# A fourth 7-product unit for the gates, and two pieces of stick-breaking attention moved off VectorE

## The chip, the cores and the metric

The kernel runs on one core of a Trainium2 chip. The metric is the device time of one execution in microseconds (us), the median of three runs: 1687.3 us before the change, 1686.08 to 1689.03. The engines are named as in the profile: PE is TensorE's matmul, PEld its weight load, DVE is VectorE, ACT is ScalarE, POOL is GpSimd, and SP is SyncE, which here only issues DMAs.

## The reference

One decoder block over 1024 tokens of width 1024. From the normed input `h`, one wide projection gives everything that attention needs, and the logits of three gates:

```
proj = einsum('bsd,de->bse', h, w_in)          # columns: sb q,k,v | fox q,k,v | f | mem q | 3 x 1024 gate logits
o_sb  = stick_breaking_attention(...)          # 8 heads of 64
o_fox = forgetting_attention(...)              # 8 heads of 64
o_mem = memory_attention(...)                  # 4 heads of 128, over 256 memory tokens
gates = sigmoid(gate_logit)                    # three of (1024 tokens, 1024)
merged = gates0 * (o_sb @ Wb_sb) + gates1 * (o_fox @ Wb_fox) + gates2 * (o_mem @ Wb_mem)
x = x + merged @ w_out                         # then a squared-ReLU MLP, 1024 -> 4096 -> 1024
```

Stick-breaking attention is strictly causal. With `z = q.k / 8`, the weight of token s for query t is `sigmoid(z[t,s])` times the product of `1 - sigmoid(z[t,j])` over s < j < t, and zero for s >= t:

```
log_rem = where(strict, log_sigmoid(-z), 0);  after = reverse_cumsum(log_rem) - log_rem
w = where(strict, exp(log_sigmoid(z) + after), 0);  out = w @ v
```

Everything is float32. The kernel splits each operand of a product into a high and a low part and multiplies in two or three passes.

## The kernel before

*The order of work.* Up to the end of attention the order is not written out by hand. A planner inside the program (`Machine`, line 184) plays the kernel through when it is built: every piece of work is an `Op` with an engine and an estimated cost, every buffer a place that a `Get` waits for, and each engine takes the ready piece with the smallest due time. What it picks is emitted at once, so each engine's instructions stand in a fixed order. Pieces marked `side=True` come only when nothing else is ready on their engine: on PE these are the 7-product units, the dense gates and the branch products. DMAs are issued by SP and POOL in the same way.

*The projection.* Six projections (stick-breaking k, q and v, memory q, forgetting k and q) and the gates in `GATES` run as 7-product units (`unit_products`, `unit_evict`, line 1456): a block of 512 columns of `w_in` against both token halves is computed by Strassen's scheme with 7 half-size products instead of 8. Each product is 2 halves x 4 k x 3 passes of matmuls over 512 columns. The weight blocks' sums and splits are made by `unit_prep` (lines 1386, 1054, 1055). `GATES` holds three units: row blocks 16 to 19, 20 to 23 and 0 to 3, of 24 blocks of 128 gate columns. The units stand one behind the other in `PROJ`.

*The dense gates.* Gate blocks that are in no unit and not computed earlier run as dense tasks (`gates`, line 1811; matmuls at line 1144): blocks 4 to 7 and 10 to 15, each 2 token halves x 8 k x 3 passes. Each needs one weight block split by ACT (line 1054) and DVE (line 1055), and two evictions with a sigmoid (line 1637, a plain copy for blocks 8 to 15). All gates are stored to `gate_scr`. These tasks follow the units and are the side work of PE while attention runs.

*Attention.* Attention begins when the last unit's products are issued (`second_part`, event `ready`). Four pairs of stick-breaking heads come first, then four pairs of forgetting heads; memory attention begins after the first pair. A head's query rows are taken in four units of two 128-row tiles. For a stick-breaking tile (`sb_tile`), per chunk of up to 512 keys: PE makes the scores into one of two score banks (lines 823, 824), on the chunk with the diagonal DVE adds a mask of 1e30 to the last 128 columns in the bank (line 834), ACT takes two sigmoids of the bank, `rho` and `beta` (lines 827, 828), and DVE scans from the right, `state = rho * state + beta`, in place over `beta` (line 843). The scores are negated, so a masked column has rho 1 and beta 0. In `unit`, PE turns the weights (line 917), ACT and DVE split them (lines 922, 924), and PE multiplies with a stationary operand that holds the high and the low part of v side by side (line 934). The result has 128 rows: 64 with the products of one part of v and 64 with those of the other. Forgetting heads copy all 128 rows out and store the halves apart, to `o_scr[1]` and `low_scr`; stick-breaking heads copy 64 rows (line 962), add the other 64 on DVE (line 963) and store one half (line 965).

*The branches.* `dense_branch` multiplies the stored attention outputs with the branch weights, also at line 1144: memory first, then stick-breaking, and the forgetting branch after the planned part. Its operands are fetched by `fetched_o` (line 1659) into tiles of the ring `RR` and split by `bring`. The memory branch's operands wait for the end of memory attention (`mem_over`); the stick-breaking ones for the loads of the last pair, and two of them for the end of the memory branch. For the forgetting branch `fetched_o` also loads the low half and the row sums. `RR` has three tiles, two of them lent to stick-breaking attention until its four pairs are over, and gets four more when all pairs are over.

Of the kernel before, what the change touches and what calls it, by code (L numbers as in the profile page):

```python
# [27 lines left out]
HD = 64  # L28
# [15 lines left out]
def tile_hybrid_block(  # L44
# [20 lines left out]
    nc = tc.nc  # L65
# [20 lines left out]
    dram = ctx.enter_context(tc.tile_pool(name="dram", bufs=1, space=bass.MemoryType.DRAM))  # L86
# [24 lines left out]
        nc.scalar.activation(C.t("st", [P, 8])[:, :1], one, AF.Sqrt)  # L111
    root_table()
    o_scr = [dram.tile([512, S], F32, name=f"o_scr{b}", tag=f"o_scr{b}") for b in range(3)]
    low_scr = dram.tile([512, S], F32, name="low_scr", tag="low_scr")
    l_scr = dram.tile([8, S], F32, name="l_scr", tag="l_scr")
    gate_scr = dram.tile([3 * D, S], F32, name="gate_scr", tag="gate_scr")
    fq_scr = dram.tile([8, 4, S], F32, name="fq_scr", tag="fq_scr")
# [219 lines left out]
    holder = {}  # L337
# [6 lines left out]
    def banks(tag):  # L344
        return Places([bank(tag) for _ in range(PSB[tag])])
# [4 lines left out]
    PP, SC, TR, PV = (banks(tag) for tag in ("pp", "sc", "tr", "pv"))  # L350
    ES, OO, EL, RR, HT, PH, PL, OB, VV, BK, LATER, NONE, RQ = (Places([]) for _ in range(13))
# [460 lines left out]
    def sb_tile(pair, b, i, beta):  # L812
        n = P * (i + 1)
        q = pair.t["q", b, i // 4][:, (i % 4) * P:(i % 4 + 1) * P]
        ch = chunks(i)
        scanned = Event()

        def chunk(ci, c, m, u):
            rho = yield Get(RQ)
            sc = yield Get(SC)  # L820

            def scores():
                nc.tensor.matmul(sc[:, :m], q, pair.t["k1", b, ci][:, :m], start=True, stop=False)
                nc.tensor.matmul(sc[:, :m], q, pair.t["k2", b, ci][:, :m], start=False, stop=True)

            def sigmoids():
                nc.scalar.activation(rho[:, :u], sc[:, :u], AF.Sigmoid, scale=HD ** -0.5)
                nc.scalar.activation(beta[:, c:c + u], sc[:, :u], AF.Sigmoid, scale=-HD ** -0.5)  # L828

            yield Op("PE", 2 * mm_time(max(m, 256)), scores)  # L830
            last = c + u == n
            if last:
                dg = sc[:, u - P:u]
                yield Op("DVE", 0.22, lambda: nc.vector.tensor_tensor(
                    dg, dg, holder["later"][:, 385:513], ALU.add))
            yield Op("ACT", act_time(u, u), sigmoids, table=AF.Sigmoid)
            SC.put(sc)
            if not last:
                yield scanned

            def scan():
                back = beta[:, c:c + u][:, ::-1]
                nc.vector.tensor_tensor_scan(out=back, data0=rho[:, :u][:, ::-1], data1=back,  # L843
                                             initial=0.0 if last else beta[:, c + u:c + u + 1],
                                             op0=ALU.mult, op1=ALU.add)
# [42 lines left out]
    def unit(pair, b, g, es):  # L888
# [2 lines left out]
        for ev in [spawn(tile_(pair, b, 2 * g + a, es[a]), 0.5 * a) for a in range(2)]:  # L891
            yield ev
        pair.read(b, g)
        scr, r0 = o_scr[0 if pair.kind == "sb" else 1], (2 * pair.p + b) * HD
        js = list(range(2 * g + 1, -1, -1))
        turned, pv, started = [], [None], Event()
        products = [Event() for _ in range(g + 2)]
# [51 lines left out]
            yield ev  # L949
        ob = yield Get(OB)  # L950
        rows, cols = slice(r0, r0 + HD), slice(g * 256, (g + 1) * 256)
        if pair.kind == "fox":
            yield Op("ACT", act_time(256), lambda: nc.scalar.activation(ob, pv[0][:, :256], AF.Copy))
            PV.put(pv[0])

            def halves():
                nc.sync.dma_start(scr[rows, cols], ob[:HD, :])
                nc.sync.dma_start(low_scr[rows, cols], ob[HD:, :])
            yield Op("SP", 0.2, halves, 3.0)
        else:  # L960
            o = ob[:HD, :]
            yield Op("ACT", act_time(256), lambda: nc.scalar.activation(o, pv[0][HD:P, :256], AF.Copy))
            yield Op("DVE", dve_time(256), lambda: nc.vector.tensor_tensor(o, o, pv[0][0:HD, :256], ALU.add))
            PV.put(pv[0])
            yield Op("SP", 0.1, lambda: nc.sync.dma_start(scr[rows, cols], o), 2.5)
        OB.put(ob)
        pair.units += 1
        if pair.units == 8:
# [383 lines left out]
        machine.fire(forgot)  # L1352

    KINDS = ("P1", "P2", "P6", "P7", "P5", "P3", "P4")
    GATES = {"ga": 16, "gb": 20, "gc": 0}
    PROJ = ("sbk", "sbq", "mq", "fxk", "fxq", "sbv", *GATES)
    COLS = {**{u: C_G + n * P for u, n in GATES.items()}, "sbv": C_SBV, "mq": C_MQ, "fxk": C_FXK, "fxq": C_FXQ, "sbk": C_SBK, "sbq": C_SBQ}
    prepped, p_ops, landed_ = ({(u, kind): Event() for u in PROJ for kind in KINDS} for _ in range(3))
# [160 lines left out]
    def unit_final(u, ct, q, src, of_bank=False):  # L1519

        c, t = ct
        if u == "sbv":
# [135 lines left out]

    def fetched_o(bi, k):

        raw_ = yield Get(RR)
        raw, rows = raw_[:, :S], slice(k * P, (k + 1) * P)
        yield from transfer(lambda: nc.sync.dma_start(raw, o_scr[order[bi][1]][rows, :]), P * S * 4)
        if bi == 2:
            t = yield Get(RR)
            yield from transfer(lambda: nc.sync.dma_start(t, low_scr[rows, :]), P * S * 4)
            yield Sleep(1.0 if k == ks[3] else 2.0)
            yield Op("DVE", dve_time(S), lambda: nc.vector.tensor_tensor(raw, raw, t, ALU.add))
# [278 lines left out]
    for s in range(0, ST, 2):  # L1947
        t = RA.t("h", [P, 2, D])
# [3 lines left out]
    gb = N.t("gb", [P, D])  # L1952
# [54 lines left out]
    sb = []  # L2007
# [34 lines left out]
    with tc.manual_schedule():  # L2042
# [79 lines left out]
        rows = [], []  # L2122
# [598 lines left out]
```

## Time and profile before

| | us |
|---|---|
| runs: median, lowest, highest | 1687.3, 1686.08, 1689.03 |
| profiled execution, first to last instruction | 1686.7 |
| PE busy | 1675.3 |
| DVE, ACT, POOL busy | 1293.0, 848.9, 255.2 |
| last 7-product unit | 441.7 to 480.6 |
| stick-breaking and memory attention | 480.6 to 719 |
| forgetting attention | 719 to 877.8 |
| stick-breaking branch | 877.8 to 922.5 |

The profile is of one execution; its time is its span, which lies within the runs. Times in it count from its first instruction. Busy time of a group is the union of its instructions, so groups whose matmuls overlap can't be added; a number behind an x is a count. An idle time is put down to what ended it.

### The profile page before, as it was taken

What the parts mean: (1) busy time and instruction counts of PE and PEld (TensorE: products, weight loads), DVE (VectorE), ACT (ScalarE), POOL (GpSimd) and SP (SyncE); (2) the same over time, 40 slices, a digit from 0 to 9 for tenths busy, and PEclk for the clock granted to TensorE, in tenths of its full rate; (3) what the DMA queues carried; (4) which work ended last, traced back from release to release, by engine and by line L of the source; (5) the groups of instructions that cost most, each with busy time, mean ns of one, the idle gap of its engine ahead of it and who ended that gap; (6) DMA issues with size and microseconds to landing.
All of it is one profiled execution on the core that took longest, in us unless ns stands there. A gap on an engine that the chain in (4) does not pass through costs nothing.

```text
span 1686.7 us, 25003 instructions
## 1 busy us (share of the span) xinstructions
PE 1675.3 (99%) x9118; PEld 1432.0 (85%) x9118; DVE 1293.0 (77%) x2079; ACT 848.9 (50%) x1474; POOL 255.2 (15%) x440
## 2 busy tenths in 40 slices
PE   9999999999999999999999999999999999999999
PEld 9998899998888888888888887878888887888887
DVE  7977778855459888867877898987777776688775
ACT  6455555534358888866761446433333344332331
POOL 0000000000253151254400011022111120000000
PEclk9999999999999999999999999999999999999999
DMA  7445434467475365387747542144444484564532
GB/s 245 157 150 182 149 119 150 146 194 243 127 232 161 111 186 151 117 240 224 236 146 245 183 162 100 57 162 155 152 150 137 150 307 171 202 202 143 198 125 75
DMA packets 142221, 284.32 MB, mean 169 GB/s; under 512 B 16913, under 2 KB 53329, under 8 KB 142098
## 3 DMA queue, kind: packets, MB, share of 16 engines
q1 hardware_dynamic: 110562, 183.08, 32.0%
q0 software_dynamic: 31536, 99.64, 19.5%
q8 instruction: 72, 1.18, 0.3%
q14 instruction: 51, 0.42, 0.1%
HBM read 189.83 MB, written 92.83 MB: 168 GB/s over the span
## 4 chain that ended last, share of the span: by engine, by line
PE 92%; DVE 5%; DMA 2%; ACT 1%; issue 1%; SPq 0%; DVEq 0%; ACTq 0%
PE pp L1456 11%; PE pp L1144 10%; PE pp L1981 10%; PE pp L2658 8%; PE sc L1456 7%; PE sc L1144 6%; PE sc L1981 5%; PE sc L2658 4%; PE tr L2658 4%; PE tr L917 4%; PE pv L1456 3%; PE pv L2658 3%; PE tr L1981 2%; PE sc L934 2%; PE pp L934 2%; DVE h L1917 1%
## 5 line engine op out<-in xcount | busy, mean ns | idle before, releaser
L1055 DVE TENSOR_TENSOR wlo<-raw,whi 128x1024 fp32r<-128x1024 f32 (+1 forms) x88 | 107.5, 1222 | 80.2 <-ACT whi L1054 80.0
L1054 ACT ACTIVATE whi<-raw 128x1024 fp32r<-128x1024 f32 (+1 forms) x88 | 93.2, 1059 | 78.8 <-PE pp L1456 32.7
L2658 PE MATMUL pp<-h,sop 128*128 128x512 f32 x540 | 128.4, 396 | 0.0
L2658 PEld LDWEIGHTS pp<-h,sop 128*128 128x128 f32 x540 | 101.6, 188 | 24.4
L1981 PE MATMUL pp<-h,oh 128*128 128x512 f32 x384 | 121.1, 397 | 0.7 <-ACT cu L2066 0.6
L924 DVE TENSOR_TENSOR ptl<-tr,pth 128x512 fp32r<-128x512 f32 (+1 forms) x160 | 99.1, 628 | 24.1 <-ACT pth L922 23.1
L922 ACT ACTIVATE pth<-tr 128x512 fp32r<-128x512 f32 (+1 forms) x160 | 87.4, 556 | 36.0 <-PE sc L934 15.8
L1981 PEld LDWEIGHTS pp<-h,oh 128*128 128x128 f32 x384 | 72.0, 188 | 19.0 <-ACT cu L2066 1.4
L2573 ACT ACTIVATE h<-t 128x2048 fp32r<-128x2048 f32 (+1 forms) x17 | 30.7, 1814 | 110.2 <-DVE t L1917 97.4
L1373 POOL DMA_DIRECT2D raw<-w_in x32 | 24.2, 755 | 395.1 <-DVE wlo L1055 395.1
L1144 PE MATMUL sc<-h,whi 128*128 128x512 f32 (+1 forms) x254 | 77.7, 389 | 0.0
L1456 PE MATMUL pp<-h,whi 128*128 128x512 f32 x248 | 77.5, 394 | 0.0
L1981 PE MATMUL pp<-h,ol 128*128 128x512 f32 x192 | 76.1, 396 | 0.0
L1456 PE MATMUL pp<-whi,h 128*128 128x256 f32 x384 | 71.8, 283 | 0.0
L843 DVE TENSOR_TENSOR_SCAN e<-r,e 128x384 f32<-128x384 f32 (+3 forms) x64 | 66.3, 1044 | 6.9 <-ACT e L828 6.5
L1974 ACT ACTIVATE oh<-raw 128x512 fp32r<-128x512 f32 x64 | 39.4, 625 | 61.8 <-DVE raw L1917 61.8
L2658 PE MATMUL sc<-h,sop 128*128 128x512 f32 x264 | 63.7, 396 | 0.0
L2658 PE MATMUL tr<-h,sop 128*128 128x512 f32 x264 | 63.4, 396 | 0.0
L1917 DVE TENSOR_TENSOR sop<-ur,sop 128x2048 fp32r<-128x2048 f32 (+1 forms) x28 | 61.8, 2211 | 2.0 <-ACT sop L2586 2.0
L917 PE MATMUL tr<-ident,e 128*128 128x128 f32 x416 | 62.7, 273 | 0.0
L1456 PEld LDWEIGHTS pp<-whi,h 128*128 128x128 f32 x384 | 60.2, 188 | 0.0
L2658 PEld LDWEIGHTS sc<-h,sop 128*128 128x128 f32 x264 | 49.6, 188 | 12.3 <-DVE sop L1917 0.5
(558 smaller groups left out, 5087.7 us busy)
## 6 DMA issues: line engine op xcount, KB each, us to landing
ur<-s_scr SPq DMA_DIRECT2D x26, 1024.0 KB
raw<-w_in POOLq DMA_DIRECT2D x42, 512.0 KB, 4.9
raw<-w_up SPq DMA_DIRECT2D x60, 256.0 KB
s_scr<-s POOLq DMA_DIRECT2D x60, 256.0 KB, 2.7
g<-w_down SPq DMA_DIRECT2D x14, 1024.0 KB
s_scr<-cu POOLq DMA_DIRECT2D x48, 256.0 KB, 2.8
h<-sbk_scr POOLq DMA_DIRECT2D x64, 128.0 KB, 3.2
o<-gate_scr SPq DMA_DIRECT2D x32, 256.0 KB
```

The source lines that it names most:

```text
L843: nc.vector.tensor_tensor_scan(out=back, data0=rho[:, :u][:, ::-1], data1=back, initial=0.0 if last else beta[:, c + u:c + u + 1], op0=ALU ...
L917: nc.tensor.transpose(tr[:, jj * 256 + a * P:jj * 256 + (a + 1) * P], es[a][:, j * P:(j + 1) * P], ident)
L922: yield Op("ACT", act_time(512 - lo_c), lambda: nc.scalar.activation(ph[:, lo_c:], tr[:, lo_c:], AF.Copy))
L924: yield Op("DVE", dve_time(512 - lo_c), lambda: nc.vector.tensor_tensor(pl[:, lo_c:], tr[:, lo_c:], f32(ph[:, lo_c:]), ALU.subtract))
L934: nc.tensor.matmul(pv[0][:, c_:256], pair.v[:, j, b, :], p_[:, jj * 256 + c_:(jj + 1) * 256], start=(k == 0 and n_ == 0 and i == 0), stop= ...
L1054: yield Op("ACT", 0.03 + act_time(m), lambda: nc.scalar.activation(hi, raw, AF.Copy))
L1055: yield Op("DVE", dve_time(m), lambda: nc.vector.tensor_tensor(lo, raw, f32(hi), ALU.subtract))
L1144: nc.tensor.matmul(ps, a_, b_, start=(first and i == 0), stop=(last and i == n - 1))
L1456: nc.tensor.matmul(out_, a_, b_, start=(first and n == 0 and j == 0), stop=(last and n == 3 and j == len(todo) - 1), skip_group_check=True)
L1917: nc.vector.tensor_tensor(out_, a_, b_, op)
L1981: nc.tensor.matmul(ps, w[a_][:, k * P:(k + 1) * P], h[b_][k], start=(first and k == 0 and i == 0), stop=(last and k == 3 and i == 2), skip ...
L2658: nc.tensor.matmul(ps, a_[:, c, qs], b_[:, c, :], start=(kind in ("P1", "P2", "P7") and c == 0 and i == 0), stop=(kind in ("P2", "P4", "P3 ...
```

## The change

It has three parts. Gate blocks 4 to 7 become a fourth unit of `GATES` behind the third, and their four dense tasks disappear. In `sb_tile` the mask add on DVE goes; ACT takes `beta` before `rho`, and after both POOL writes zeros into the masked part of the last 128 columns of `beta` with an affine select, ahead of the scan. `rho` stays unmasked: the scan starts from 0, and while beta is 0 the state stays 0. In `unit`, stick-breaking heads are evicted as the forgetting heads are: all 128 rows copied by ACT, and both halves stored by SP, the second to a scratch tensor of its own. `fetched_o` loads this second half for the stick-breaking branch, into a second tile of `RR` that it asks for together with the first, and DVE adds the two.

```diff
-    low_scr = dram.tile([512, S], F32, name="low_scr", tag="low_scr")
+    low_scr = [dram.tile([512, S], F32, name=f"low_scr{b}", tag=f"low_scr{b}") for b in range(2)]
...
             def sigmoids():
+                nc.scalar.activation(beta[:, c:c + u], sc[:, :u], AF.Sigmoid, scale=-HD ** -0.5)
                 nc.scalar.activation(rho[:, :u], sc[:, :u], AF.Sigmoid, scale=HD ** -0.5)
-                nc.scalar.activation(beta[:, c:c + u], sc[:, :u], AF.Sigmoid, scale=-HD ** -0.5)
...
-            if last:
-                dg = sc[:, u - P:u]
-                yield Op("DVE", 0.22, lambda: nc.vector.tensor_tensor(
-                    dg, dg, holder["later"][:, 385:513], ALU.add))
             yield Op("ACT", act_time(u, u), sigmoids, table=AF.Sigmoid)
             SC.put(sc)
-            if not last:
+            if last:
+                dg = beta[:, n - P:n]
+                yield Op("POOL", 0.3, lambda: nc.gpsimd.affine_select(
+                    out=dg, in_=dg, pattern=[[-1, P]], compare_op=ALU.is_ge, fill=0.0, base=-1, channel_multiplier=1))
+            else:
                 yield scanned
...
-        if pair.kind == "fox":
-            yield Op("ACT", act_time(256), lambda: nc.scalar.activation(ob, pv[0][:, :256], AF.Copy))
-            PV.put(pv[0])
-
-            def halves():
-                nc.sync.dma_start(scr[rows, cols], ob[:HD, :])
-                nc.sync.dma_start(low_scr[rows, cols], ob[HD:, :])
-            yield Op("SP", 0.2, halves, 3.0)
-        else:
-            o = ob[:HD, :]
-            yield Op("ACT", act_time(256), lambda: nc.scalar.activation(o, pv[0][HD:P, :256], AF.Copy))
-            yield Op("DVE", dve_time(256), lambda: nc.vector.tensor_tensor(o, o, pv[0][0:HD, :256], ALU.add))
-            PV.put(pv[0])
-            yield Op("SP", 0.1, lambda: nc.sync.dma_start(scr[rows, cols], o), 2.5)
+        yield Op("ACT", act_time(256), lambda: nc.scalar.activation(ob, pv[0][:, :256], AF.Copy))
+        PV.put(pv[0])
+
+        def halves():
+            nc.sync.dma_start(scr[rows, cols], ob[:HD, :])
+            nc.sync.dma_start(low[rows, cols], ob[HD:, :])
+        yield Op("SP", 0.2, halves, 3.0)
...
-    GATES = {"ga": 16, "gb": 20, "gc": 0}
+    GATES = {"ga": 16, "gb": 20, "gc": 0, "gd": 4}
...
-        raw_ = yield Get(RR)
+        raw_, *low_ = (yield Get(RR, 2)) if bi == 1 else [(yield Get(RR))]
...
+        if bi == 1:
+            t = low_[0]
+            yield from transfer(lambda: nc.sync.dma_start(t, low_scr[0][rows, :]), P * S * 4)
+            yield Op("DVE", dve_time(S), lambda: nc.vector.tensor_tensor(raw, raw, t, ALU.add))
+            RR.put(t)
```

More of the change, by code (lines that the diff above doesn't have):

```diff
@@ L893, in unit @@
         pair.read(b, g)
-        scr, r0 = o_scr[0 if pair.kind == "sb" else 1], (2 * pair.p + b) * HD
+        of_sb = pair.kind == "sb"
+        scr, low, r0 = o_scr[0 if of_sb else 1], low_scr[0 if of_sb else 1], (2 * pair.p + b) * HD
         js = list(range(2 * g + 1, -1, -1))
@@ L1659, in fetched_o @@
     def fetched_o(bi, k):
-        raw_ = yield Get(RR)
+        raw_, *low_ = (yield Get(RR, 2)) if bi == 1 else [(yield Get(RR))]
         raw, rows = raw_[:, :S], slice(k * P, (k + 1) * P)
         yield from transfer(lambda: nc.sync.dma_start(raw, o_scr[order[bi][1]][rows, :]), P * S * 4)
+        if bi == 1:
[3 more added lines that the diff above has]
+            RR.put(t)
         if bi == 2:
             t = yield Get(RR)
-            yield from transfer(lambda: nc.sync.dma_start(t, low_scr[rows, :]), P * S * 4)
+            yield from transfer(lambda: nc.sync.dma_start(t, low_scr[1][rows, :]), P * S * 4)
             yield Sleep(1.0 if k == ks[3] else 2.0)
```

## The prediction

> **What bounds the kernel now.** I read the page first, then the busy times by stage, then the groups of instructions inside the stage that the change touches. The page:
>
> ```profile
> span 1686.7 us, 25003 instructions
> PE 1675.3 (99%) x9118; PEld 1432.0 (85%) x9118; DVE 1293.0 (77%) x2079; ACT 848.9 (50%) x1474; POOL 255.2 (15%) x440
> PE 92%; DVE 5%; DMA 2%; ACT 1%; issue 1%; SPq 0%; DVEq 0%; ACTq 0%
> ```
>
> TensorE (PE) is busy for 99% of the span, and 92% of the chain that ended last runs on it. So the kernel's time is its PE work plus whatever time PE stands still. The question is whether PE can stay full after work is moved. The stages give that; each row is the stretch, its length, then the busy us of PE, PEld, DVE, ACT and POOL with their instructions, the granted clock, the DMA share and GB/s:
>
> ```profile
> 441.70:480.60 38.90, 38.90 (x169) 31.66 (x169) 13.36 (x14) 14.29 (x20) 14.43 (x27) 1.00 0.50 160
> 480.60:719.00 238.40, 238.40 (x1471) 209.89 (x1470) 204.40 (x380) 202.38 (x446) 74.09 (x133) 1.00 0.52 154
> 500.00:550.00 50.00, 50.00 (x313) 44.12 (x312) 46.59 (x80) 40.79 (x93) 16.84 (x30) 1.00 0.59 178
> 550.00:600.00 50.00, 50.00 (x317) 44.41 (x316) 41.54 (x75) 43.57 (x98) 9.10 (x17) 1.00 0.33 103
> 600.00:650.00 50.00, 50.00 (x309) 43.85 (x308) 46.03 (x83) 44.42 (x99) 19.66 (x36) 1.00 0.67 194
> 650.00:700.00 50.00, 50.00 (x318) 44.34 (x318) 41.78 (x80) 44.96 (x99) 13.22 (x24) 1.00 0.44 132
> 719.00:740.20 21.20, 21.20 (x130) 18.42 (x128) 13.12 (x25) 13.07 (x29) 13.71 (x26) 1.00 1.00 277
> 740.20:877.80 137.60, 136.13 (x887) 120.64 (x887) 107.83 (x297) 97.70 (x227) 47.22 (x87) 0.99 0.67 203
> 877.80:922.50 44.70, 44.70 (x197) 36.33 (x196) 34.87 (x48) 9.06 (x14) 2.24 (x3) 1.00 0.70 219
> ```
>
> 441.7 to 480.6 is the last 7-product unit: PE full, DVE and ACT one third busy. 480.6 to 719 is stick-breaking attention with memory attention mixed in: PE full, but DVE and ACT also 86% and 85% busy. 719 to 877.8 is forgetting attention, 877.8 to 922.5 the second branch product alone. PE is full in the attention stages only because line 1144 fills every gap with work that belongs to nobody there, the dense gates and then the branches. The same stretches for line 1144 alone (length, PE, PEld, clock, DMA):
>
> ```profile
> 480.60:719.00 238.40, 132.19 (x480) 85.18 (x480) 1.00 0.52 154
> 719.00:740.20 21.20, 13.17 (x48) 8.46 (x49) 1.00 1.00 277
> 740.20:877.80 137.60, 55.75 (x193) 34.15 (x192) 0.99 0.67 203
> 877.80:922.50 44.70, 44.48 (x192) 35.96 (x192) 1.00 0.70 219
> ```
>
> Its PE times overlap with neighbours, so I count matmuls and take the pace from the chain of waits, where 48 products of the unit stage stand end to end:
>
> ```profile
> 425.22 11.11 PE sc L1456 x48
> ```
>
> That is 0.2315 us each. Ten dense gates are 480 matmuls (48 each by the loops: 2 halves, 8 k, 3 passes). The 48 of 719 to 740.2 are the last of them, so 432 ran before 719 (100.0 us), and the other 48 of that row are memory attention. The first branch's 192 take from 740.2 to the end of attention, the second's 192 come after it.
>
> **The change, part by part.** *Gates into a unit.* Removed from attention: 4 x 48 = 192 matmuls, 44.5 us. Added ahead of it: 7 products x 2 halves x 4 k x 3 passes = 168 matmuls, 38.9 us, the length of the unit in the first stage row. PE's own work falls by 24 matmuls, 5.6 us. The unit's loads, sums, splits and evictions are covered: in the last unit DVE and ACT were busy 13.4 and 14.3 of 38.9 us, and twice that still fits. So attention starts 38.9 us later and has 288 filler matmuls of gates left instead of 480.
>
> *DVE and ACT in attention.* What leaves the stick-breaking stage (groups in 480.6 to 719; then the gates' weight splits and evictions):
>
> ```profile
> L834 DVE TENSOR_TENSOR pv<-pv,later 128x128 f32<-128x128 f32 x38 | 10.9, 287 | 3.9 <-PE pv L824 3.7
> L834 DVE TENSOR_TENSOR pp<-pp,later 128x128 f32<-128x128 f32 x26 | 7.5, 289 | 4.4 <-PE pp L824 4.2
> L963 DVE TENSOR_TENSOR ob<-ob,sc 64x256 f32<-64x256 f32 x18 | 7.2, 400 | 2.0 <-ACT ob L962 1.9
> L963 DVE TENSOR_TENSOR ob<-ob,pp 64x256 f32<-64x256 f32 x14 | 5.6, 398 | 0.2 <-ACT ob L962 0.2
> L1055 DVE TENSOR_TENSOR wlo<-raw,whi 128x1024 fp32r<-128x1024 f32 x9 | 10.8, 1205 | 0.0
> L1054 ACT ACTIVATE whi<-raw 128x1024 fp32r<-128x1024 f32 x9 | 9.7, 1074 | 0.0
> L1637 ACT ACTIVATE o<-sc 128x512 f32<-128x512 f32 x9 | 5.6, 624 | 0.6 <-PE sc L1144 0.6
> L1637 ACT ACTIVATE o<-pp 128x512 f32<-128x512 f32 x8 | 4.9, 608 | 2.6 <-PE pp L1144 2.6
> L962 ACT ACTIVATE ob<-sc x18: 368/381/383, 501.4 to 716.7; 64x256 f32<-64x256 f32 x18
> L953 ACT ACTIVATE ob<-sc x16: 362/378/385, 727.8 to 874.4; 128x256 f32<-128x256 f32 x16
> ```
>
> DVE: 64 mask adds 18.4, 32 sums of halves 12.8, 4 splits 4.8, together 36.0 us of 204.4, so 168.4 remain. ACT: 4 splits 4.3 and 8 evictions 4.9, together 9.2 of 202.4, so 193.2 remain; the copy of 128 rows costs the same as that of 64 (378 against 381 ns). DVE is relieved a lot, ACT hardly, and ACT becomes the fuller of the two.
>
> *What POOL, SP and the branch take on.* The nearest POOL, SP and DVE rows are these:
>
> ```profile
> L1563 POOL TENSOR_SCALAR_AFFINE_SELECT later<-later 128x129 f32<-128x129 f32 x1 | 0.3, 293 | 0.1
> L1004 POOL DMA_DIRECT2D h<-sbk_scr x46 | 23.9, 527 | 64.7 <-PE pv L151 29.6 <-PE pp L824 13.2 <-PE pp L1144 9.3
> L843 DVE TENSOR_TENSOR_SCAN e<-r,e 128x384 f32<-128x384 f32 (+3 forms) x64 | 66.3, 1044 | 6.9 <-ACT e L828 6.5
> L843 DVE TENSOR_TENSOR_SCAN es<-r,es 128x128 f32<-128x128 f32 (+3 forms) x32 | 26.0, 817 | 3.8 <-ACT es L828 3.5
> L965 SPq DMA_DIRECT2D o_scr<-ob x32: 445/446/548, 502.9 to 717.6; - x32
> L1668 DVE TENSOR_TENSOR r<-r,r x3: 1214/1218/1220, 794.4 to 890.8; 128x1024 f32<-128x1024 f32 x3
> ```
>
> 64 selects of 0.293 us are 18.8 us of POOL, which is busy 74 of 238 us: they fit. Each one now stands between the sigmoids and the scan of its tile, and behind what POOL is issuing: from 0 to a burst of four loads, 4 x 0.527 = 2.1 us, during which that scan and the transposes after it wait. The mask add stood in the queue of a DVE that was 86% busy, and held the score bank meanwhile. I take the two waits as equal. SP issues 32 more stores of 0.45 us and four more loads, the branch adds four DVE sums of 1.22 us. All of it lies inside attention with DMA at about half share and must be done only when the second branch starts; today that is 877.8. Each operand now asks for two tiles of the same small ring at once, so the four loads come nearly one after another. I count nothing for it; if the cover goes, one load and one sum more per operand stand ahead of the second branch, which I bound at 0 and 8 us. The two sigmoids of a chunk only change places, which costs nothing either.
>
> *How much the stage shortens.* In the four 50 us rows the fuller of DVE and ACT is busy 46.6, 43.6, 46.0 and 45.0 of 50, mean 0.91, highest 0.93, lowest 0.87. ACT's need in these 200 us is 173.7, less 9.2 x 200/238 = 166.0 after. At the lowest density they become 190.8 us (9 shorter), at the mean 183.2 (17), at the highest 178.5 (22), at 1.0 they become 166.0 (34). With filler gone a ready attention matmul finds PE free more often, so I take the highest that was seen: 22 us shorter, and leave the ramps outside as they are. The stage lasts 238.4 - 22 = 216.4 us.
>
> PE's need in it is 238.4 - 100.0 + 288 x 0.2315 = 205.1 us. So PE runs out of filler and stands still for 216.4 - 205.1 = 11.3 us.
>
> *The gap before the first branch.* Its operands wait for the end of memory attention (719) and a trip through memory:
>
> ```profile
> 719.00:731.60 12.60, 7.64 (x28) 4.88 (x29) 1.00 0.96 277
> 730.86 0.71 DVE wlo L1055
> 731.58 8.90 DMA r<-o_scr
> 742.59 0.50 PE L869 MATMUL pv<-h,h 128*128 128x512 f32 x1 [1.47 <-DVE st L874]
> 743.80:747.10 3.30, 3.30 (x10) 2.52 (x9) 1.11 (x7) 2.05 (x4) 0.00 (x0) 0.50 0.98 338
> ```
>
> The first operand's split ends at 731.6. Until then 28 gate matmuls ran (first row, line 1144 alone); after the change none is left, and 28 x 0.2315 = 6.5 us of PE stand empty. The bounds are 0, if memory attention ends earlier, and the 11.1 us of all 48, if the last load is again slow to land (8.9 us).
>
> The last two rows show a second price of standing still: PE waited 1.47 us, and then ran 3.3 us at half the granted clock, which costs 1.65 us. I count nothing for it, as such a stretch falls where PE has room, and up to four times that, 6.6 us, for the range. The Trainium skill, "TensorE: Matmul & The Clock Gate", Part 1, says that the clock halves after an idle window of about 3.4 us. Here it halved after 1.47 us of idleness. By that rule only long gaps would pay, and the sum would stay as it is.
>
> *Sum.* -5.6 of PE work, +11.3 and +6.5 of idle PE: +12.2 us. The same by stages: +38.9 for the unit, -22 for the stage, and 11.1 - 6.5 = 4.6 us of the second branch drawn into forgetting attention: +12.3. The profiled span is 1686.7, 0.6 below the median of 1687.3, to which I add it: about 1700 us.
>
> **The rivals.** *PE stays full* (faster). The stage shortens by 33 us or more, the gap closes, and the 5.6 us arrive: 1681.7. For it: with PE at 100% in every attention row, DVE and ACT may be waiting for PE, and the sum of halves and the mask leave long chains. Against it: ACT would have to be busy 193.2 of 205.1 us, 94% over the whole stage, its ramps included. It decides from 33 us of shortening on.
>
> *Saving and gap cancel.* About 30 us shorter with half the gap: -5.6 + 3.3 + 3.2 = +1, 1688.
>
> *The relief is lost* (slower still). The select delays the scan by more than the mask add did, or ACT holds the pace: the stage shortens by only 9 us, PE idles 24.3 + 6.5: -5.6 + 30.8 = +25, 1712. For it: the 64 selects read what the scans read and write, and 96 scans fill DVE for 92 us of the stage.
>
> The Trainium skill, "SBUF — State Buffer", Who interferes with whom, says that a DVE instruction with two SBUF inputs and a GpSimd instruction that reads SBUF lock each other out. The scan and the select would be such a pair. If each of the 64 selects held up a scan for its 0.293 us, DVE would lose 18.8 of the 36.0 us of relief, and ACT would still be the fuller engine. No row before the change has the two side by side.
>
> **How the numbers follow.** Forecast 0.45, PE stays full 0.25, cancel 0.15, relief lost 0.15. I call under 0.2% (3.4 us) no change, about what runs 2.95 us apart can tell. So faster 0.25, the same 0.15, slower 0.60. The forecast's own range, with the stage 14 to 28 us shorter (+20.2 to +6.2 us) and a half-clock stretch or two, is 1693 to 1710. The whole range takes in the full 5.6 us of the first rival and the lost relief: 1681 to 1713.
>
> **What would show it.** Right: line 1456 with 168 more matmuls ending near 519.5; DVE clearly below ACT in stick-breaking; PE idle showing for the first time there, in its last third and just before the first branch, with half-clock stretches beside it; the second branch still mostly after attention. Wrong: PE at 100% through attention and ACT above 93%, or no PE idle ahead of the first branch. If selects wait long behind loads on POOL, or scans stretch beyond their 1044 ns mean, the relief was lost there.

## The result, and the profile after

The change makes the kernel slower: 1737.5 us in the median (1736.35 to 1738.8, 4 runs) against 1686.7 for the kernel before on the same chip (1684.94 to 1689.03, 4 runs). The ratio is 1.0303, with a 95% interval of 1.0289 to 1.0318, so +50.8 us. Forecast were 1700 us, +12.2 on the profiled span, with a range that ended at 1713. The sign was right; the change cost four times as much as forecast.

The page of the changed kernel, its span, busy times and chain:

```profile
span 1736.0 us, 25064 instructions
...
PE 1688.8 (97%) x9094; PEld 1433.8 (83%) x9094; DVE 1288.7 (74%) x2000; ACT 849.5 (49%) x1481; POOL 285.4 (16%) x504
...
PE 80%; issue 7%; DVE 6%; DMA 3%; POOL 2%; ACT 2%; SPq 0%; POOLq 0%; ACTq 0%; DVEq 0%
```

PE's share of the chain fell from 92% to 80%. Its work fell by 24 matmuls (9118 to 9094), yet its busy time rose by 13.5 us. The stages, with the columns as in the prediction (length, PE, PEld, DVE, ACT, POOL, clock, DMA, GB/s):

```profile
480.60:519.50 38.90, 38.90 (x169) 31.51 (x168) 13.08 (x14) 14.30 (x20) 14.32 (x26) 1.00 0.55 178
519.50:770.30 250.80, 229.07 (x1414) 198.13 (x1412) 188.95 (x311) 200.62 (x461) 115.91 (x219) 0.97 0.53 157
519.50:675.90 156.40, 155.68 (x957) 136.09 (x955) 117.29 (x167) 131.00 (x294) 69.81 (x135) 1.00 0.53 157
675.90:782.70 106.80, 81.41 (x513) 69.07 (x511) 78.90 (x164) 78.42 (x190) 53.27 (x98) 0.91 0.58 171
782.70:916.00 133.30, 130.88 (x834) 114.69 (x834) 105.99 (x276) 89.54 (x208) 40.11 (x73) 0.99 0.69 197
916.00:926.30 10.30, 2.21 (x10) 1.40 (x8) 4.34 (x7) 2.58 (x6) 0.75 (x1) 0.75 0.84 299
926.30:969.70 43.40, 43.39 (x177) 34.77 (x178) 30.64 (x41) 5.34 (x7) 1.50 (x2) 0.94 0.53 169
```

The unit takes its 38.9 us. Stick-breaking with memory attention, 519.5 to 770.3 (where the first branch's first load is issued), lasts 250.8 us. It was 238.4 before and forecast at 216.4. PE is full up to 675.9 and then not: 25.4 us idle in the next 106.8, 2.4 and 8.1 in the two rows behind. The dense gates and branch products alone, now line 1138 (length, PE, PEld, clock, DMA):

```profile
519.50:675.90 156.40, 84.20 (x312) 55.33 (x311) 1.00 0.53 157
675.90:782.70 106.80, 7.82 (x27) 4.06 (x25) 0.91 0.58 171
```

The 288 gate matmuls are used up by 675.9. The few in the second row belong to memory attention. PE's timeline has its four longest idle times of attention in brackets, each with what ended it:

```profile
686.09 0.80 PE L823 MATMUL pp<-h,h 128*128 128x512 f32 x1 [5.12 <-ACT r L828]
...
740.67 0.66 PE L918 MATMUL tr<-ident,es 128*128 128x128 f32 x2 [4.85 <-DVE ptl L925]
...
780.17 0.66 PE L918 MATMUL tr<-ident,e 128*128 128x128 f32 x4 [2.88 <-DVE ptl L925]
...
926.31 0.79 PE L1138 MATMUL pp<-h,whi 128*128 128x512 f32 x1 [8.10 <-ACT h L1048]
```

Three are attention waiting for its own chain, from ACT and DVE. The fourth is the second branch waiting for its last operand's split. The same table of stages for the stretches at half clock, which lie beside them:

```profile
682.20:692.40 10.20, 6.31 (x26) 5.61 (x27) 5.04 (x7) 7.93 (x19) 3.79 (x8) 0.50 0.57 174
...
719.80:723.20 3.40, 3.24 (x16) 2.94 (x15) 2.44 (x6) 3.39 (x7) 0.01 (x1) 0.50 0.01 2
740.20:743.60 3.40, 2.93 (x13) 2.86 (x14) 2.72 (x8) 0.80 (x3) 0.00 (x0) 0.51 0.57 133
781.20:784.60 3.40, 3.40 (x15) 3.11 (x14) 1.89 (x3) 1.64 (x3) 1.04 (x2) 0.50 1.06 275
...
921.10:931.30 10.20, 4.99 (x11) 3.68 (x12) 5.49 (x7) 1.15 (x2) 0.71 (x1) 0.50 0.84 311
...
1074.70:1078.10 3.40, 3.40 (x12) 2.67 (x11) 2.88 (x4) 3.40 (x9) 0.00 (x0) 0.51 0.53 204
```

The last row lies behind attention, where PE had stood still for 2.59 us up to 1073.49. PE worked 24.3 us in these stretches, 12.1 of which it would have saved at full clock (before: 1.65). The 49.3 us of span then come to: -5.6 of work, +35.8 of idle (49.3 less the 13.5 of busy time; 35.1 of it lie in the stages above), +10.5 of half clock, and some 9 in which PE counts as busy without doing more. A likely reading of these 9, which no run tests, is that short bursts lose the overlap of one matmul with the next: the profile gives a 128x512 product 0.39 us, but 48 in a row take 11.1 us, 0.23 each.

Two places deserve a look. The first is POOL's timeline of the changed kernel where a pair is loaded:

```profile
670.24 0.29 POOL L836 TENSOR_SCALAR_AFFINE_SELECT es<-es 128x128 f32<-128x128 f32 x1 [2.33 <-ACT es L827]
670.71 4.15 POOL L998 DMA_DIRECT2D h<-sbk_scr  x8 [0.18 <-issue]
674.85 1.04 POOL L998 DMA_DIRECT2D h<-sbq_scr  x2
675.88 0.79 POOL L1056 DMA_DIRECT2D raw<-w_b  x1
676.66 1.05 POOL L998 DMA_DIRECT2D h<-sbq_scr  x2
677.72 1.19 POOL L836 TENSOR_SCALAR_AFFINE_SELECT es<-es 128x128 f32<-128x128 f32 x3
...
735.62 1.18 POOL L836 TENSOR_SCALAR_AFFINE_SELECT es<-es 128x128 f32<-128x128 f32 x3
```

And ACT's timeline from there on:

```profile
677.20 0.60 ACT L923 ACTIVATE pth<-tr 128x512 fp32r<-128x512 f32 x1 [0.29 <-PE pv L935]
684.47 0.60 ACT L701 ACTIVATE o<-pp 128x512 f32<-128x512 f32 x1 [6.67 <-DMA gate_scr<-o]
```

Thirteen issues in a row hold POOL for 7.0 us, and three selects behind them run together at the end. ACT then stands 6.67 us at the head of its queue for a tile whose store, issued at 676.08, is slow to land beside those loads, and the sigmoids behind it wait with it: that is the 5.12 us of PE at 686. In a run below with the same order but no selects, POOL has issued the same loads by 667.7, and ACT waits 2.43 us at this place. The longest row of issues comes later: seventeen, 9.2 us, from 726.38 to the last line. A scan stands 2.62 us for the three selects there, and PE's stop of 4.85 us ends with the transposes of `es` tiles behind it.

The second is the fetch of the second branch's operands, in SP's timeline the loads of the high halves (line 1657) and of the low ones (line 1660):

```profile
874.33 0.45 SPq L1657 DMA_DIRECT2D r<-o_scr  x1
...
879.97 0.53 SPq L1660 DMA_DIRECT2D r<-low_scr  x1
...
887.17 0.40 SPq L1657 DMA_DIRECT2D r<-o_scr  x1
...
893.91 0.54 SPq L1660 DMA_DIRECT2D r<-low_scr  x1
...
902.34 0.38 SPq L1657 DMA_DIRECT2D r<-o_scr  x1
...
907.31 0.58 SPq L1660 DMA_DIRECT2D r<-low_scr  x1
...
917.18 0.89 SPq L1657 DMA_DIRECT2D r<-o_scr  x2
...
918.96 0.41 SPq L1660 DMA_DIRECT2D r<-low_scr  x1
```

The sums on DVE as a group (shortest, median and longest in ns, first and last start):

```profile
L1661 DVE TENSOR_TENSOR r<-r,r x4: 1215/1220/1226, 883.8 to 924.4; 128x1024 f32<-128x1024 f32 x4
```

One operand follows the other at 13 to 15 us, and the last sum starts at 924.4, when PE has stood still since 926.31 - 8.10 = 918.2.

### The profile page after: what moved, and what is told of

It reads as the page before. It is cut to its first block, busy times and chain, and to the rows that moved or that the text cites. A ratio compares the mean times of both kernels' runs of the same rounds, so it can differ in the third digit from the quotient of the medians.

```text
span 1736.0 us, 25064 instructions
## 1 busy us (share of the span) xinstructions
PE 1688.8 (97%) x9094; PEld 1433.8 (83%) x9094; DVE 1288.7 (74%) x2000; ACT 849.5 (49%) x1481; POOL 285.4 (16%) x504
## 4 chain that ended last, share of the span: by engine, by line
PE 80%; issue 7%; DVE 6%; DMA 3%; POOL 2%; ACT 2%; SPq 0%; POOLq 0%; ACTq 0%; DVEq 0%
PE pp L1450 11%; PE pp L1138 8%; PE sc L1450 8%; PE pp L1980 7%; PE pp L2657 7%; PE sc L1138 5%; PE tr L2657 4%; PE sc L2657 4%; PE pv L1450 3%; PE sc L1980 3%; PE tr L918 3%; PE pv L2657 2%; PE pv L935 2%; PE tr L1980 2%; PE pp L935 1%
## 5 line engine op out<-in xcount | busy, mean ns | idle before, releaser
L925 DVE TENSOR_TENSOR ptl<-tr,pth 128x512 fp32r<-128x512 f32 (+1 forms) x160 | 99.5, 630 | 39.9 <-ACT pth L923 38.9
L1450 PE MATMUL pp<-h,whi 128*128 128x512 f32 x296 | 92.5, 394 | 0.0
L918 PE MATMUL tr<-ident,e 128*128 128x128 f32 x416 | 65.1, 278 | 11.6 <-DVE ptl L925 11.1
L843 DVE TENSOR_TENSOR_SCAN e<-r,e 128x512 f32<-128x512 f32 (+3 forms) x64 | 65.6, 1044 | 13.9 <-ACT r L828 9.8
L918 PEld LDWEIGHTS tr<-ident,e 128*128 128x128 f32 x416 | 50.0, 142 | 24.3 <-DVE ptl L925 16.5
L1138 PE MATMUL pp<-h,whi 128*128 128x512 f32 x192 | 62.0, 403 | 8.1 <-ACT h L1048 8.1
L1973 ACT ACTIVATE oh<-raw 128x512 fp32r<-128x512 f32 x64 | 39.5, 625 | 61.8 <-DVE raw L1916 61.8
L1450 PEld LDWEIGHTS pp<-h,whi 128*128 128x128 f32 x296 | 55.6, 188 | 13.0
```

The source lines that it names most:

```text
L918: nc.tensor.transpose(tr[:, jj * 256 + a * P:jj * 256 + (a + 1) * P], es[a][:, j * P:(j + 1) * P], ident)
L925: yield Op("DVE", dve_time(512 - lo_c), lambda: nc.vector.tensor_tensor(pl[:, lo_c:], tr[:, lo_c:], f32(ph[:, lo_c:]), ALU.subtract))
L1138: nc.tensor.matmul(ps, a_, b_, start=(first and i == 0), stop=(last and i == n - 1))
L1450: nc.tensor.matmul(out_, a_, b_, start=(first and n == 0 and j == 0), stop=(last and n == 3 and j == len(todo) - 1), skip_group_check=True)
```

## The experiments

Three theories were tried. A: attention lacks filler, because 44.5 us of gate products left it and its pace is set by ACT, DVE and their chains. B: the select on POOL makes the stage long. C: the second branch's operands come late. Each difference below is to the kernel before on the same chip in the same comparison (1685.9 to 1686.3).

**Gates alone.**

```diff
-    GATES = {"ga": 16, "gb": 20, "gc": 0}
+    GATES = {"ga": 16, "gb": 20, "gc": 0, "gd": 4}
```

> The gates alone: gates 4 to 7 in a fourth 7-product unit, mask and output halves as in the kernel before. Theory A (too little filler): the PE work falls by 5.6 us, but 44.5 us of products that filled the stick-breaking stage are gone and the stage's pace is set by ACT, DVE and the chains between them; nearly all the loss comes from this part, 1715 to 1735 us, with 30 us or more of PE idle in attention. Theory B (the select on POOL queued behind load issues makes the stage long): without the select the stage keeps its pace or gains; the gates alone cost at most what was forecast for an unshortened stage, 1700 us or less, PE idle under 20 us. Theory C (the two-tile fetch of the second branch) puts 8.1 us of idle and up to 5 us of half clock of the loss elsewhere, so this kernel should be about 10 us under the changed one by it: 1727 or less.

Measured: 1721.1, +34.9 (ratio 1.0208, 1.0191 to 1.0225). A stretch of its stage, and the stage, in the same columns:

```profile
700.00:750.00 50.00, 41.41 (x262) 34.01 (x260) 43.11 (x98) 41.70 (x100) 16.28 (x31) 0.97 0.33 102
519.60:769.80 250.20, 232.57 (x1436) 198.99 (x1434) 213.97 (x419) 209.21 (x474) 81.67 (x151) 0.99 0.48 144
```

The stage is as long as in the whole change, with none of its other parts. The time falls where A has it; the 30 us of idle that it also named were 24.7 (519.6 to 916).

**Mask alone, halves alone, both.** Against the kernel before, the hunks of the change that concern the mask (order of the sigmoids, the select in place of the add), the output halves (store, second load, sum), and the two together:

```diff
# mask
-                yield Op("DVE", 0.22, lambda: nc.vector.tensor_tensor(dg, dg, holder["later"][:, 385:513], ALU.add))
+                yield Op("POOL", 0.3, lambda: nc.gpsimd.affine_select(out=dg, in_=dg, ...))
# halves
-            yield Op("DVE", dve_time(256), lambda: nc.vector.tensor_tensor(o, o, pv[0][0:HD, :256], ALU.add))
+            nc.sync.dma_start(low[rows, cols], ob[HD:, :])
```

> The mask alone: zeros by a select on POOL in place of the add on DVE, gates and halves as before. Theory A: with the filler still there, PE stays full; the time stays within 3 us of before (1684 to 1690). Theory B: the selects behind POOL's load bursts (five bursts' worth of 4 to 10 us each in the changed kernel) stretch the stage, which can show as PE idle in spite of the filler: 1692 to 1705.

> The output halves alone: both halves stored and added ahead of the second branch, gates and mask as before. Theory A: within 3 us of before. Theory C (two tiles fetched one after the other, so the fourth pair of operands comes late): about 8 us of PE idle at the second branch's operands and up to 5 us of half clock behind it, 1694 to 1700.

> Mask and halves together, the gates as before. Theory A: with the filler there both are hidden, 1683 to 1690. B and C: the sum of what the two cost alone, 1694 to 1715.

Measured: mask 1696.1, +9.9 (1.0062, 1.0047 to 1.0077); halves 1703.4, +17.3 (1.0103, 1.0088 to 1.0118); both 1711.1, +24.9 (1.0147, 1.0132 to 1.0162). Neither is hidden, even with all the filler there, so A alone isn't enough. With the halves alone PE waits for the second branch's operands, as its timeline shows:

```profile
886.08 0.80 PE L1138 MATMUL sc<-whi,whi 128*128 128x512 f32 x1 [8.26 <-ACT whi L1048]
...
892.68 1.52 PE L1138 MATMUL sc<-h,whi 128*128 128x512 f32 x2 [4.65 <-ACT h L1048]
```

The stretch around it, in the columns of the stages:

```profile
881.50:898.50 17.00, 7.77 (x16) 5.11 (x17) 9.55 (x12) 2.30 (x4) 0.00 (x0) 0.50 0.78 286
```

That is 12.9 us of idle and 3.9 us of half clock, 16.8 of 17.3. With the mask alone the order of the work is another one. Loads of the forgetting pairs are issued on POOL early, the first at 653.38 (670.14 in the kernel before), and the next ones wait there for tiles that scores of forgetting heads still read (POOL's waits in 650 to 770: us, times, longest):

```profile
POOL h L1004 <- PE pv L870: 47.5, 4, 18.0
```

The kernel before has such waits too, one of 18.83 us at 691.08. The first branch's first product runs at 769.02 (740.27 before), and PE's timeline has these two stops beside it:

```profile
768.12 0.66 PE L917 MATMUL tr<-ident,es 128*128 128x128 f32 x4 [3.11 <-DVE ptl L924]
...
771.88 0.58 PE L934 MATMUL pp<-pth,v 128*128 128x256 f32 x1 [1.53 <-ACT pth L922]
```

Whether the new order or the select itself makes the 9.9 us was not tested for this kernel.

**Gates and halves**, the mask as before.

> Gates and halves, the mask added on DVE as before. If the parts add up as they did alone (gates +34.9, halves +17.3 us over a before of 1686.2): 1738, as slow as the whole change, and the select then costs nothing on top. If the select is what makes the whole change slow (theory B): 10 us or more under the changed kernel, 1727 or less. The second branch's operands should again come late by about 8 us (theory C), since nothing of their fetch is undone.

Measured: 1724.4, +38.2 (1.0227, 1.0212 to 1.0242). The halves cost 17.3 alone and only 3.3 on top of the gates, so with little filler their relief of DVE is worth something. The operands of the second branch come late again, by 8.99 and 3.49 us of PE idle. The mask's move costs the remaining 12.6.

**The whole change, operands through single tiles.**

```diff
-        raw_, *low_ = (yield Get(RR, 2)) if bi == 1 else [(yield Get(RR))]
+        raw_ = yield Get(RR)
...
-            t = low_[0]
+            t = yield Get(LOWT)                  # one tile, kept for the four low halves
...
-            if i == 2:
+            if i >= 1:
                 yield branches[0].done
```

> The whole change, but the second branch's operands no longer take two tiles at once: one tile is kept for the low halves, the raw tiles are taken singly, and the third branch's second operand is fetched only after the first branch, so that its tile is free. Theory C: the 8.1 us of PE idle at 926 us and most of the 10.2 us of half clock around it go, 1725 to 1731. If the operands are late for another reason (the stores of the last pairs, the splits), the time stays at 1737 and the idle is still there.

Measured: 1725.7, +39.5 (1.0237, 1.022 to 1.0254). The fetch cost 11.3 us. The end of attention and the second branch, with single tiles and then in the whole change as it was:

```profile
900.00:950.00 50.00, 49.45 (x240) 40.75 (x239) 34.81 (x49) 12.14 (x21) 2.99 (x4) 1.00 0.71 225
```

```profile
900.00:950.00 50.00, 41.91 (x202) 34.26 (x202) 34.85 (x49) 14.05 (x26) 2.11 (x3) 0.90 0.64 207
```

PE is busy 49.45 us of 50 in place of 41.91, and at full clock.

**The whole change without a mask.**

```diff
-                yield Op("POOL", 0.3, lambda: nc.gpsimd.affine_select(...))
-            else:
+            if not last:
                 yield scanned
```

> The whole change with the diagonal mask left out altogether: neither the select on POOL nor an add on DVE, so the diagonal blocks of the stick-breaking weights keep entries that the reference has as zeros. This bounds what the select costs by its waits (78 us summed over 64 selects) and by its place on POOL. Theory B (selects behind parked load issues lengthen the stage): 1717 to 1728, and the stage from the end of the unit to the first load of the first branch's operands falls well under the 250.8 us of the changed kernel, to 240 or less. Theory A (no filler, the stage goes at the pace of ACT, DVE and their chains): 1733 to 1740, the stage still 247 us or more.

Measured: 1713.2, +27.0 (1.0162, 1.0147 to 1.0177). B holds for the time: the select costs 23.8 us. Its other sign, a shorter stage, doesn't show: the first load of the first branch is issued at 769.2, since forgetting attention mixes into the stage earlier. The 78 us of waits named there stand in no row as such: in the changed kernel POOL is idle for 77.2 us ahead of the 32 selects on `e` and 39.3 ahead of those on `es`, nearly all of it waiting for a sigmoid, and DVE is idle for 9.2 us ahead of scans that wait for selects (lines in the last section).

**Gates alone, and gates 4 to 7 a second time as dense tasks.**

```diff
-... if n // 4 * 4 not in GATES.values()]
+... if n // 4 * 4 not in (0, 16, 20)]
```

> The gates alone as in the run with only the gates (1721.1), but gates 4 to 7 are computed a second time as four dense gates in the old place, so that the 192 matmuls (44.5 us) of filler are back in attention, with their evictions and stores; the outputs are the same. Theory A (holes that only lack filler): the holes take the extra work, 0 to 8 us more than without, 1721 to 1729, PE idle in attention under 5 us and no half clock there but one window. If the holes were due to something that filler cannot cover (a hand-over, a queue), the extra work comes on top: 1745 to 1766.

Measured: 1724.9, +38.6 (1.023, 1.0215 to 1.0245), 3.7 more than without. PE in the stretch shown for the gates alone is full again:

```profile
700.00:750.00 50.00, 50.00 (x307) 43.83 (x306) 41.39 (x83) 43.41 (x96) 12.33 (x22) 1.00 0.43 129
```

The time is now the kernel before's plus the unit's 38.9 us. Taking 44.5 us of products out of attention again saves only 3.7: the rest turns into holes, which these products had filled. A is shown, for this part.

**The whole change, selects ahead of loads on POOL; the pairs' loads on SP.** The first gives the select the earliest due time and makes each load of a pair a step of its own. The second:

```diff
-                        nc.gpsimd.dma_start(f32(t[k][rows_, :]), src)
+                        nc.sync.dma_start(f32(t[k][rows_, :]), src)
```

> The whole change, with the same work, but POOL's program is ordered anew: the loads of a pair are issued one by one, not four as one step, and a select goes ahead of every load that is not yet issued. Leaving the select out gave 24 us. Theory B1 (the select is late because it stands behind load issues of 0.53 us each on POOL): most of that comes back, 1715 to 1725, and the stall of 5.1 us on PE at 686 goes. Theory B2 (the select costs by its own duration beside the scans, and as one more step in a chain that nothing covers once the filler is gone): the order changes little, 1731 to 1740.

> The whole change, but the loads of the pairs (queries, keys) are issued by SP, so that POOL keeps only the selects, the values, the memory operands and the weights. Theory B1: 1713 to 1725, since almost nothing is left ahead of a select. Theory B2: 1731 to 1740. A third way: the loads now stand behind SP's stores that wait for their tiles, the pairs come late and the time rises over 1740.

Measured: 1730.3, +44.4 (1.0261, 1.0245 to 1.0276), and 1743.4, +57.5 (1.0338, 1.0323 to 1.0353). Going first on POOL gives back 6.4 of the 23.8 us (with another order of the programs, too), just more than B2 allowed and less than B1 asked. The stop of 5.1 us at 686 did go, and no PE stop of 2 us is left ahead of 768.3; part of the gain is lost at the second branch's operands, where PE now stands 11.1 us. On SP the third way came true: PE waits 2.40 us for a pair's queries up to 744.31. That run doesn't separate the select from late loads.

**Gates alone, dense gate 9 moved into attention.**

```diff
-    h_tasks += [dense_gate(9), *kv_tasks]
+    h_tasks += kv_tasks                         # and 9 into the list of the other gates
```

> The gates alone (1721.1), and one dense gate (number 9, 48 matmuls, 11.1 us) moved from ahead of the units into attention, behind the others, as filler. Theory A: the holes of attention take its 11.1 us, so the time falls by what the early part gets shorter, up to 11: 1710 to 1716. If the early part does not get shorter without it (PE then waits there for the first unit's operands), the time stays at 1719 to 1722 and the idle moves ahead of the units.

Measured: 1716.2, +30.4 (1.0181, 1.0164 to 1.0198). 4.5 of the 11.1 us came back, the right way, with a time just outside what was expected. The last unit ends 9.3 us earlier (its last product starts at 509.9, not 519.2), so about half of that is lost again behind it.

**Halves alone, single tiles**, the same edit as above on the halves alone.

> The halves alone (1703.4, with 12.9 us of PE idle ahead of the second branch's operands and 17.1 us of half clock) with the fetch changed as in the run of the whole change with single tiles. Theory C: the halves then cost next to nothing while the filler is there, 1685 to 1691. If the stores of the low halves or the add on DVE cost by themselves: 1695 or more.

Measured: 1687.1, +1.3 (1.0006, 0.9997 to 1.0015). All of the halves' price was the fetch.

**The whole change's order, the selects left out; the selects on spare data.**

```diff
# the order kept
-                yield Op("POOL", 0.3, lambda: nc.gpsimd.affine_select(out=dg, in_=dg, ...))
+                yield Op("POOL", 0.3, lambda: None)
# on spare data, and no scan waits for it
-                dg = beta[:, n - P:n]
-                yield Op("POOL", 0.3, ...)
+                dg = holder["later"][:, :P]
+                spawn(aside())                   # the same select
```

> The whole change with each engine's program in exactly its order, but the 64 selects left out of POOL's program, so that the diagonal blocks keep entries that the reference has as zeros. If the select itself costs (its wait on POOL, its step between sigmoid and scan, its hold on the port): near the run without it, 1712 to 1720. If the cost is the order that the programs get when a tile's chain has one more step: near the whole change, 1730 to 1737.

> The whole change with 64 selects of the same size on POOL, but on a spare tile that the scans do not read, so that no scan waits for one; the diagonal blocks are not masked. If the select costs because it stands in the chain ahead of the scan (its step or its wait): as without it, 1711 to 1718. If it costs by the port that it shares with DVE: 1722 or more.

Measured: 1726.8, +40.8 (1.024, 1.0223 to 1.0257), between the two answers; and 1712.3, +26.2 (1.0156, 1.0141 to 1.0171), as without selects. So the 23.8 us fall in two. 10.0 go with the select itself, its wait on POOL and its step ahead of the scan; these two, and the loads that a waiting select holds up, are not told apart. 13.8 are the order that the planner writes when the chain of a tile has a step more. The stick-breaking scores of one bank as a group (duration, then first and last start, then shapes) show the two orders, for the run with the change's order and, below it, the one without a mask:

```profile
L823 PE MATMUL pp<-h,h x49: 280/396/775, 522.5 to 719.7; 128*128 128x512 f32 x37, 128*128 128x256 f32 x8, 128*128 128x384 f32 x2, 128*128 128x128 f32 x2
```

```profile
L823 PE MATMUL pp<-h,h x48: 223/392/481, 522.3 to 694.3; 128*128 128x512 f32 x33, 128*128 128x256 f32 x8, 128*128 128x128 f32 x4, 128*128 128x384 f32 x3
```

Neither has a select to run, and in one the stick-breaking scores end 25 us earlier. The first has the changed kernel's shapes in this bank (37, 8, 2 and 2).

**Both mends, and the best with the unit.** The whole change with the selects first and single tiles; and gates, halves through single tiles, gate 9 in attention, the mask on DVE. The edits are those above.

> The whole change with both mends: selects ahead of load issues, issued one by one, and the second branch's operands through single tiles. If they add up (7.2 and 11.8 us off 1737.5): 1718.5. The trace of the run with the selects first shows 11.1 us of idle and 17.1 us of half clock at the second branch's operands, more than the 8.1 and 10.2 of the whole change, so it may come to 1713 to 1718.

> The best that these runs suggest with the unit: gates in a fourth unit, mask added on DVE as before, halves stored apart and fetched through single tiles, dense gate 9 moved into attention. From the gates and halves (1724.4) less about 12 for the fetch and 5 for gate 9: 1707 (1701 to 1713). Theory A says that it cannot come under 1686, since the holes of attention still lack some 30 us of filler.

Measured: 1717.5, +31.4 (1.0186, 1.0171 to 1.0201), so the two mends add up (6.4 and 11.3 us alone, 19.4 together); and 1708.0, +21.9 (1.0131, 1.0115 to 1.0146). No version with the unit comes near the kernel before.

## Why the prediction was wrong

Two terms carry the miss: the select, whose wait was taken as equal to that of the mask add (it cost 23.8 us, 10.0 by itself and 13.8 by the new order), and the hand-over of the second branch's operands, counted at nothing (11.3 us). With the forecast's +12.2, a relief 2.3 short and gates 0.7 dearer, as worked out below, they come to +50.3, against +50.8 measured.

**What held.** The bound was read rightly: PE's fullness rests on filler. The unit cost 38.9 us, the 192 matmuls left attention, and the first idle showed in the stage's last third and ahead of the first branch, though the longest stop came ahead of the second. DVE fell below ACT (188.95 against 200.62 us in the stage). The prediction's own arithmetic with no shortening at all, -5.6 of work, 238.4 - 205.1 = 33.3 of idle and 6.5 of gap, gives +34.2. The gates alone cost +34.9. The total agrees better than its parts: the stage got 11.8 us longer, PE's idle time grew by 23.1 us where this sum has 39.8, and its busy time grew by 9.5 where the sum has -5.6. So the closeness is partly luck.

**"22 us shorter".** This term was near as a relief and wrong as a net. Taking the add off DVE, with no select in its place, was worth 11.2 us (1724.4 to 1713.2), and the halves, with the mended fetch, 8.5 (+30.4 to +21.9, with gate 9 moved): together 19.7. What it didn't hold is what takes the add's place. The way it was derived failed too: attention without filler did not run at the highest density seen before. The fuller of DVE and ACT was busy 86% of the stage with the gates alone and 80% in the changed kernel, where 93% was taken, and the stage took 250.8 us, not 216.4. The relief shows in the total time, not in that stage.

**"I take the two waits as equal", 0 to 2.1 us each.** This is the step that failed most: 23.8 us. A burst on POOL isn't four loads but up to seventeen issues, 9.2 us, because the planner writes several steps one behind the other. Only 6.4 us are the place on POOL, though, or 8.1 with the fetch mended (+39.5 to +31.4). The larger part wasn't in the prediction in any form: it took the order of the programs as given, and an `Op` more in a chain changes what the planner writes for all engines.

**The hand-over, counted at nothing, bound 8.** Measured 11.3. The 8.1 us of idle is the bound's very number, which is luck: runs with the same fetch show 7.8 to 12.9. The half clock behind it and the knock-on weren't in it. The note that the four loads come nearly one after another was right, and should have been priced: 13 to 15 us each against a first branch that leaves PE empty at 918.

**Half clock, counted at nothing, bound 6.6.** 10.5 us more than before. The Trainium skill, "TensorE: Matmul & The Clock Gate", Part 1, gives a free-running window of 3413 ns. The stretches here are whole multiples of 3.4 us, which agrees. So do their starts in the changed kernel (682.2, 719.8, 740.2, 781.2, 921.1 and 1074.7), which lie 11, 17, 29, 70 and 115 steps of 3.413 us behind the first. That only long gaps pay isn't borne out: 2.59 and 2.88 us of idle sufficed. Nor does the length of one gap decide alone: no half clock followed the 1.66 us up to 733.39, and one followed the 1.47 us in the kernel before.

Along the chain of runs: gates +34.9, halves +3.3, mask off DVE -11.2, select +23.8, together +50.8. This adds up by construction. What checks it is that the +3.3 is about -8.5 + 11.3 = 2.8, from other runs. What stays open is why the one order is 13.8 us worse: by the edits only what the planner writes differs, but which displaced piece costs the time is not shown.

## What to carry to other kernels

Where low-priority products keep an engine full, making some of them cheaper by moving them elsewhere can cost their whole length, as here, unless the stage they leave can run faster. Price such a change first with no speed-up at all, and then ask for each relieved engine what takes the removed step's place. Before a short instruction goes to a queue that issues DMAs, look in the timeline for the longest run of issues there, not at one; and where a planner writes the order, a step put into a chain is a change to every engine's program.

## What was not expected of the hardware

The clock falls after the idle time, not only in it. PE waited 2.88 us up to 780.17, and the half clock ran from 781.2 to 784.6, where PE was busy 3.40 of 3.40 us. So the price fell on full work.

The select hardly stretched the scans. The scans on the two kinds of tile and the selects on the first, in the changed kernel, with busy us and mean ns behind the bar:

```profile
L843 DVE TENSOR_TENSOR_SCAN e<-r,e 128x512 f32<-128x512 f32 (+3 forms) x64 | 65.6, 1044 | 13.9 <-ACT r L828 9.8 <-POOL e L836 3.8
...
L843 DVE TENSOR_TENSOR_SCAN es<-r,es 128x128 f32<-128x128 f32 (+3 forms) x32 | 26.2, 833 | 7.8 <-POOL es L836 5.4 <-ACT r L828 2.3
...
L836 POOL TENSOR_SCALAR_AFFINE_SELECT e<-e 128x128 f32<-128x128 f32 x32 | 16.3, 515 | 77.2 <-ACT e L827 75.2 <-DVE e L843 1.9
```

The same selects' shortest, median and longest:

```profile
L836 POOL TENSOR_SCALAR_AFFINE_SELECT e<-e x32: 284/298/1631, 523.3 to 723.2; 128x128 f32<-128x128 f32 x32
```

The scans' mean is 1044 ns on `e`, as before, and 833 on `es` (817 before). The selects on `e` take 298 ns in the median but up to 1631. One that began just after a scan ended with it, as DVE's and POOL's timeline shows:

```profile
725.07 1.27 DVE L843 TENSOR_TENSOR_SCAN e<-r,e 128x512 f32<-128x512 f32 x1
...
725.10 1.33 POOL L836 TENSOR_SCALAR_AFFINE_SELECT es<-es 128x128 f32<-128x128 f32 x1 [1.62 <-ACT es L827]
```

The Trainium skill, "SBUF — State Buffer", Who interferes with whom, says that issue order decides whether a DVE or a GpSimd instruction is blocked where the two contend. The trace agrees here: the select came 0.03 us later and took 1.33 us. Yet 64 selects on spare data cost no time that could be measured (1712.3 against 1713.2).
